# Seven block products for eight in twelve pairs of column groups of a float32 decoder layer

## The chip, the core and the metric

The kernel runs on one core of one Trainium2 chip, in one launch. The metric is the device time of that launch in microseconds (us). TensorE (PE in the profile; PEld is its weight load) multiplies, VectorE (DVE), ScalarE (ACT) and GpSimd (POOL) do the rest, and SyncE (SP) issues nearly all DMAs. Each engine takes its instructions in the order in which they were written; engines wait for each other through semaphores.

## The reference, cut to what matters

One decoder layer for 256 tokens of width 2048, in float32. All large products have the 256 tokens on one side and a weight matrix on the other; the change touches the products for the three gates (3 x 2048 of the columns of `w_in`) and for the SwiGLU input (`w_ffn_in`, 2 x 5632 columns).

```python
h = rms_norm(x, g_pre_mix)
proj = h @ w_in                                  # q, k, v, indexer, ..., gate_logits
o_a = dsa_attention(...); o_b = retention(...); o_c = memory_attention(...)
gates = sigmoid(gate_logits).reshape(B, S, 3, D)
mixed = gates[..0] * (o_a @ w_branch_a) + gates[..1] * (o_b @ w_branch_b) + gates[..2] * (o_c @ w_branch_c)
x = x + rms_norm(mixed @ w_out, g_post_mix)
h2 = rms_norm(x, g_pre_ffn)
f_gate, f_up = split(h2 @ w_ffn_in)
x = x + rms_norm((silu(f_gate) * f_up) @ w_ffn_out, g_post_ffn)
```

## The kernel before

**The split.** A float32 product is made of three products of a shorter type (fp32r): each operand is cut into a high part and a low part (the rest), and x.w = xh.wh + xh.wl + xl.wh. The activations are cut once (`Operand.hi`, `Operand.lo`, transposed, k in the partitions); the weights are cut as they stream past.

**Jobs, chunks, units.** `jobs` is one list of column groups, mostly 512 columns wide, in the order of the program. A job (`Job`, L71) takes `kt` blocks of 128 in k: 16 for a projection of width 2048, 8 for the branches a and c, 44 for the last product. A chunk is four of these blocks, 1 MB of weights, loaded by one DMA into a `raw` tile (three buffers, L127). A unit is half a chunk: ScalarE casts 128x1024 weights to `whi` (L140), VectorE subtracts to get `wlo` (L146), and TensorE does twelve matmuls of 512 columns: two k blocks times two halves of the tokens times three products (L204 to L206), into the job's two accumulators of a PSUM bank each.

**Order.** The instruction order is written out by hand by `Stream.run` (L150): ahead of unit s it writes the casts up to unit s+3 and the subtractions up to unit s+2 (`for kind, ahead in ((his, 3), (los, 2))`, L178), casts first. `whi` and `wlo` have four buffers each, so a cast for unit s+3 writes over what unit s-1 has read. After each unit, `tick` (L112) takes one step of each of two queues of side work: `fast`, the evacuations of the jobs' accumulators, and `slow`, everything else (attention, retention, residual). `until` (L118) takes as many steps as are needed where a unit needs something that has not been written yet. `turned` (L367) transposes an evacuated group through VectorE's 32x32 transposes, eight small DMAs to DRAM and one back, and two more steps some units later; `transpose_split` (L414) does it with TensorE transposes.

**What stands around the change.** Order of the jobs: four of the memory, three of the indexer, two each of aq, ak, av, mq, rq and rk (all with xs, the normalised tokens); then ga 0, branch a 0, ga 1, branch a 1, and so on to 3; the same with gc and branch c; four times rg and rv (retention, each followed by `retain` in the slow queue); gb and branch b; four of `w_out`; then eleven times a gate and an up group of the SwiGLU (`ffn_gate` L1028, `ffn_up` L1039; xop is h2), and four of `w_ffn_out`. The evacuation of a merge (L755) takes two multiplications with a bank and two additions; that of rk (`roped_T`, `rope` L468) four operations per half of the tokens and a `turned`. `make_h2` (L958) makes h2 beside the first SwiGLU job and then puts `residual` (L1002, six steps) into the slow queue. PSUM is two pools of four banks: the jobs' accumulators (`acc`) and all else (`aux`).

```python
for kind, ahead in ((his, 3), (los, 2)):
    h = len(kind)
    if h >= 2 * loaded or h > s + ahead or (kind is los and h >= len(his)):
        continue
    if h > s and h >= 4 and last_use[h - 4] > n - 1:
        continue
```

Of the kernel before, what the change touches and what calls it, by code (L numbers as in the profile page):

```python
# [19 lines left out]
P = 128  # L20
D = 2048
S = 256
# [6 lines left out]
NF = DFF // 512  # L29
TOPK = 64  # L30
# [24 lines left out]
class Operand:  # L55


    def __init__(self):
        self.hi, self.lo, self.ready = [], [], set()
# [29 lines left out]

class Stream:  # L90


    def __init__(self, nc, wr, ws, acc, nm):
        self.nc, self.wr, self.ws, self.acc, self.nm = nc, wr, ws, acc, nm
        self.fast, self.slow = deque(), deque()
        self.now, self.calls = 0, []

# [29 lines left out]
    def load(self, job, c, pieces):  # L127
        raw = self.wr.tile([P, 4, job.nw], F32, tag="raw", name=self.nm("raw"))
        flat = raw.rearrange("p a b -> p (a b)")
        n = 4 * job.nw // pieces  # L130
        for k in range(pieces):
            if 2 * k % pieces == 0:
                job.xop.load(c, 2 * k // pieces)
            self.nc.sync.dma_start(flat[:, k * n:(k + 1) * n], job.w[c][:, k * n:(k + 1) * n])
        return raw

    def high(self, raw, hf, nw, pieces=1):
        hi = self.ws.tile([P, 2, nw], F32R, tag="whi", name=self.nm("whi"))
        for sl in ([slice(0, 2)] if pieces == 1 else [slice(0, 1), slice(1, 2)]):
            self.nc.scalar.copy(hi[:, sl], raw[:, 2 * hf + sl.start:2 * hf + sl.stop])  # L140
        return hi

    def low(self, raw, hf, nw, hi, pieces=1):
        lo = self.ws.tile([P, 2, nw], F32R, tag="wlo", name=self.nm("wlo"))
        for sl in ([slice(0, 2)] if pieces == 1 else [slice(0, 1), slice(1, 2)]):
            self.nc.vector.tensor_sub(lo[:, sl], raw[:, 2 * hf + sl.start:2 * hf + sl.stop],  # L146
                                      hi[:, sl].bitcast(F32))
        return lo

    def run(self, jobs):  # L150
        PE = self.nc.tensor
        chunks = [(j, c) for j in jobs for c in range(j.kt // 4)]
        units = []
        base = 0
        for j in jobs:
            nch = j.kt // 4
            c = 0
            while c < nch:
                both = (j.lead == "first" and c == 0) or (j.lead == "last" and c == nch - 2)
                for group in ([(0,), (1,)] if both else [(0, 1)]):  # L160
                    for cc in range(c, c + 2 if both else c + 1):
                        for hf in range(2):
                            units.append((j, cc, hf, group, 2 * (base + cc) + hf))
                c += 2 if both else 1
            base += nch
        last_use = {u[4]: n for n, u in enumerate(units)}
        raws, his, los, order = {}, {}, {}, []
        loaded = 0
        for n, (j, c, hf, group, s) in enumerate(units):
            while loaded < len(chunks) and loaded <= s // 2 + 3:  # L170
                if loaded >= 3 and 2 * (loaded - 3) + 1 >= len(los):
                    break
                raws[loaded] = self.load(*chunks[loaded], (4, 2, 2, 2)[loaded] if loaded < 4 else 1)
                loaded += 1
            more = True
            while more:
                more = False
                for kind, ahead in ((his, 3), (los, 2)):  # L178
                    h = len(kind)
                    if h >= 2 * loaded or h > s + ahead or (kind is los and h >= len(his)):  # L180
                        continue
                    if h > s and h >= 4 and last_use[h - 4] > n - 1:
                        continue
                    jj, cc = chunks[h // 2]
                    raw = raws[h // 2]
                    if kind is los:
                        los[h] = self.low(raw, h % 2, jj.nw, his[h], 2 if h < 2 else 1)
                    else:
                        jj.xop.ahead(cc, h % 2)
                        his[h] = self.high(raw, h % 2, jj.nw, 2 if h < 2 else 1)  # L190
                    more = True
            if c == 0 and hf == 0 and 0 in group:
                self.until(lambda: len(order) < 2 or order[-2].done)
                order.append(j)
                j.ps = [self.acc.tile([P, j.nw], F32, tag="acc", name=self.nm("acc")) for _ in range(2)]
            self.until(lambda: all((c, m) in j.xop.ready for m in group))
            hi, lo = his[s], los[s]
            for q in range(2):
                k = 4 * c + 2 * hf + q
                first, last = k == 0, k == j.kt - 1  # L200
                for m in group:
                    xh = j.xop.hi[c][:, 2 * hf + q, m * P:(m + 1) * P]
                    xl = j.xop.lo[c][:, 2 * hf + q, m * P:(m + 1) * P]
                    PE.matmul(j.ps[m], xh, hi[:, q], start=first, stop=False)  # L204
                    PE.matmul(j.ps[m], xh, lo[:, q], start=False, stop=False)  # L205
                    PE.matmul(j.ps[m], xl, hi[:, q], start=False, stop=last)  # L206
            if k == j.kt - 1:
                if j.per_m:
                    for m in group:
# [966 lines left out]
```

## Time and profile before

| | us |
|---|---|
| median of 3 runs | 1894.98 (1894.8 to 1895.67) |
| the profiled execution, its own time | 1893.63 |
| its span, from the first to the last instruction | 1891.9 |
| TensorE busy in it | 1879.8 |
| VectorE busy | 1084.8 |
| ScalarE busy | 850.8 |

The profile is one execution, recorded by the hardware. Busy is the time in which an engine had an instruction of its own running; matmuls overlap, so the distance between the starts of two of them, not their duration, is what one costs. Idle time is put down to whatever ended it.

### The profile page before, as it was taken

What the parts mean: (1) busy time and instruction counts of PE and PEld (TensorE: products, weight loads), DVE (VectorE), ACT (ScalarE), POOL (GpSimd) and SP (SyncE); (2) the same over time, 40 slices, a digit from 0 to 9 for tenths busy, and PEclk for the clock granted to TensorE, in tenths of its full rate; (3) what the DMA queues carried; (4) which work ended last, traced back from release to release, by engine and by line L of the source; (5) the groups of instructions that cost most, each with busy time, mean ns of one, the idle gap of its engine ahead of it and who ended that gap; (6) DMA issues with size and microseconds to landing.
All of it is one profiled execution on the core that took longest, in us unless ns stands there. A gap on an engine that the chain in (4) does not pass through costs nothing.

```text
span 1891.9 us, 21493 instructions
## 1 busy us (share of the span) xinstructions
PE 1879.8 (99%) x8436; PEld 1555.0 (82%) x8436; DVE 1084.8 (57%) x1308; ACT 850.8 (45%) x994; POOL 26.9 (1%) x41
## 2 busy tenths in 40 slices
PE   9999999999999999999999999999999999999998
PEld 7888878888888888888888887888888888888886
DVE  5666767765445554555555666655555555544444
ACT  7634444545444444444444444544444444444442
POOL 0000000000000000000100000000000000000000
PEclk9999999999999999999999999999999999999999
DMA  9857656555555556555566664666566666665553
GB/s 345 300 185 253 229 196 219 184 186 199 190 198 192 191 195 223 195 197 199 202 220 233 221 224 157 227 217 222 206 217 223 214 214 230 220 215 197 200 185 127
DMA packets 98134, 399.54 MB, mean 211 GB/s; under 512 B 11104, under 2 KB 43360, under 8 KB 56560
## 3 DMA queue, kind: packets, MB, share of 16 engines
q1 hardware_dynamic: 96864, 394.97, 59.4%
q0 software_dynamic: 1024, 3.18, 0.7%
q8 instruction: 66, 1.08, 0.2%
q14 instruction: 36, 0.29, 0.0%
q10 hardware_dynamic: 144, 0.01, 0.0%
HBM read 379.77 MB, written 18.35 MB: 210 GB/s over the span
## 4 chain that ended last, share of the span: by engine, by line
PE 97%; DVE 1%; DMA 1%; issue 0%; ACT 0%; POOL 0%; POOLq 0%; DVEq 0%; SPq 0%; ACTq 0%
PE acc L204 31%; PE acc L205 31%; PE acc L206 31%; DMA raw<-in_w_iq 1%; DVE wlo L146 0%; PE bk L697 0%; PE bk L715 0%; PE bk L589 0%; PE bk L662 0%; DMA raw<-in_w_mem_kv 0%; PE bk L682 0%; PE bk L816 0%; PE bk L815 0%; PE bk L814 0%; PE bk L802 0%
## 5 line engine op out<-in xcount | busy, mean ns | idle before, releaser
L146 DVE TENSOR_TENSOR wlo<-raw,whi 128x1024 fp32r<-128x1024 f32 (+2 forms) x674 | 810.5, 1208 | 557.4 <-ACT whi L140 555.7
L140 ACT CAST whi<-raw 128x1024 fp32r<-128x1024 f32 (+2 forms) x674 | 701.9, 1042 | 887.2 <-PE acc L206 822.1
L204 PE MATMUL acc<-whi,hi 128*128 128x512 f32 (+2 forms) x2688 | 1049.0, 390 | 0.4 <-ACT whi L140 0.4
L205 PE MATMUL acc<-wlo,hi 128*128 128x512 f32 (+2 forms) x2688 | 1041.6, 388 | 0.7 <-DVE wlo L146 0.6
L206 PE MATMUL acc<-whi,lo 128*128 128x512 f32 (+2 forms) x2688 | 1041.4, 387 | 0.0
L204 PEld LDWEIGHTS acc<-whi,hi 128*128 128x128 f32 x2688 | 505.5, 188 | 104.1 <-ACT whi L140 1.3
L205 PEld LDWEIGHTS acc<-wlo,hi 128*128 128x128 f32 x2688 | 505.4, 188 | 103.5 <-DVE wlo L146 2.6
L206 PEld LDWEIGHTS acc<-whi,lo 128*128 128x128 f32 x2688 | 505.1, 188 | 103.0
L412 DVE TENSOR_TENSOR lo<-turned,hi 128x1024 fp32r<-128x1024 f32 x17 | 20.8, 1226 | 42.0 <-ACT hi L411 39.0
L759 DVE TENSOR_TENSOR gate<-gate,acc 128x512 f32<-128x512 f32 x24 | 16.4, 684 | 29.3 <-PE acc L206 29.3
L1043 DVE SCALAR_TENSOR_TENSOR fg<-acc,rstd,fg 128x512 f32<-128x512 f32 x22 | 16.5, 748 | 26.8 <-PE acc L206 26.8
L477 DVE TENSOR_TENSOR rp<-acc,cos 128x512 f32<-128x512 f32 (+2 forms) x24 | 14.5, 604 | 21.8 <-PE acc L206 21.8
L825 POOL TENSOR_TENSOR rs<-ve,mhalf 128x2 f32<-128x2 f32 x8 | 12.5, 1557 | 814.0 <-DVE ve L823 814.0
L750 ACT ACTIVATE gate<-acc,rstd 128x512 f32<-128x512 f32 x24 | 16.5, 686 | 9.9 <-PE acc L206 9.9
L363 ACT CAST hi<-bk 128x512 fp32r<-128x512 f32 x12 | 7.1, 588 | 29.3 <-PE bk L715 11.6
L1034 ACT ACTIVATE fg<-acc,rstd 128x512 f32<-128x512 f32 x22 | 15.1, 686 | 9.9 <-PE acc L206 9.9
L411 ACT CAST hi<-turned 128x1024 fp32r<-128x1024 f32 x17 | 17.8, 1046 | 0.0
L365 DVE TENSOR_TENSOR lo<-bk,hi 128x512 fp32r<-128x512 f32 x12 | 8.3, 688 | 15.5 <-ACT hi L363 15.5
L594 ACT ACTIVATE rel<-bk 128x256 f32<-128x256 f32 (+1 forms) x16 | 7.9, 494 | 18.2 <-PE bk L589 18.2
L806 DVE TENSOR_TENSOR sT<-bk,dec 128x256 f32<-128x256 f32 x8 | 3.4, 424 | 21.8 <-PE bk L803 21.8
L820 DVE BATCH_NORM_STATS2 bst<-bk 128x6 f32<-128x256 f32 x16 | 6.7, 416 | 15.3 <-PE bk L816 15.3
L478 DVE TENSOR_TENSOR rp<-acc,sin 128x512 f32<-128x512 f32 (+2 forms) x24 | 14.4, 598 | 0.0
(156 smaller groups left out, 468.4 us busy)
## 6 DMA issues: line engine op xcount, KB each, us to landing
raw<-in_w_in SPq DMA_DIRECT2D x132, 1024.0 KB, 4.8
raw<-in_w_ffn_in SPq DMA_DIRECT2D x88, 1024.0 KB, 4.8
raw<-in_w_ffn_out SPq DMA_DIRECT2D x44, 1024.0 KB, 4.8
raw<-in_w_branch_b SPq DMA_DIRECT2D x16, 1024.0 KB, 5.3
raw<-in_w_out SPq DMA_DIRECT2D x16, 1024.0 KB, 4.8
d<-y SPq DMA_DIRECT2D x248, 64.0 KB, 3.1
turned<-d SPq DMA_DIRECT2D x31, 512.0 KB, 5.5
raw<-in_w_mem_kv SPq DMA_DIRECT2D x12, 1024.0 KB, 7.2
```

What stands on the lines that cost most here:

```text
L140: self.nc.scalar.copy(hi[:, sl], raw[:, 2 * hf + sl.start:2 * hf + sl.stop])
L146: self.nc.vector.tensor_sub(lo[:, sl], raw[:, 2 * hf + sl.start:2 * hf + sl.stop], hi[:, sl].bitcast(F32))
L204: PE.matmul(j.ps[m], xh, hi[:, q], start=first, stop=False)
L205: PE.matmul(j.ps[m], xh, lo[:, q], start=False, stop=False)
L206: PE.matmul(j.ps[m], xl, hi[:, q], start=False, stop=last)
L411: A.copy(h4, v)
L412: V.tensor_sub(l4, v, h4.bitcast(F32))
L477: V.tensor_tensor(t1, s4, cos, op=ALU.mult)
L750: A.activation(t[:, m], ps[m], AF.Sigmoid, scale=rms["x"][:, m:m + 1])
L759: V.tensor_tensor(g[:, m], g[:, m], ps[m], op=ALU.mult)
L1034: A.activation(t[m], ps[m], AF.Silu, scale=rmt["ffn", m])
L1043: V.scalar_tensor_tensor(t[m], ps[m], rmt["ffn", m], t[m], op0=ALU.mult, op1=ALU.mult)
```

## The change

Two neighbouring column groups are made one `Pair`. In one of its four chunks (the first, `cs` = 0), the product is seen as 2 x 2 blocks: two halves of the tokens by two halves of the chunk's k, times two halves of k by the two column groups. Eight block products of six matmuls become seven, by Strassen's scheme in Winograd's form; the other three chunks go as before. `make_forms` makes the four sums of the activations' blocks and cuts them into high and low parts, once for xs and once for h2. The sums of the weights (`t2`, `t3`, `t4`) are made by VectorE in the raw tiles when their high part is cut, and each product is one block of six matmuls into one of four accumulators W, Z, Y, X. Products that belong to two results are shared by copying an accumulator to SBUF while it goes on growing (`snapshot`, ScalarE); `finish` adds the copy to the accumulator (VectorE) and hands the sum to the old evacuation.

Pairs are ga 0 and 1, ga 2 and 3, the same of gc and gb, and gate and up group of SwiGLU 1 to 6. The merges of two groups now follow the pair. A block counts half a unit for the side queues. Raw buffers go from three to five, the pool of working tiles from 32 to 31, the two PSUM pools become one of eight, the third group merged with branch b is transposed by TensorE, and the DMA scratch is set to 4096.

```diff
+BLOCKS = range(1, 7)
...
+    def plan_pair(self, pr):
+        (j1, j2), xop, cs = pr.jobs, pr.xop, pr.cs
+        nch = j1.kt // 4
+        nc, V, A = self.nc, self.nc.vector, self.nc.scalar
+        loads = {(g, c): Load(j.w[c], 512) for g, j in enumerate(pr.jobs) for c in range(nch)}
+        r1, r2 = loads[0, cs], loads[1, cs]
+        rest = [(c, hf) for c in range(nch) if c != cs for hf in range(2)]
+        n = 6 * len(rest)
+        acc = {"W": Acc(j1, 6 + n), "Z": Acc(j1, 6 + n), "Y": Acc(j2, 12 + n), "X": Acc(j2, 18 + n)}
+        used, keep = {}, {}
+        def t2():
+            V.tensor_sub(r1.half(0), r2.half(0), r1.half(0))
+            keep["u"] = self.T([P, 2, 512], n="sum")
+            V.tensor_sub(keep["u"], r2.half(1), r1.half(0))
+            return keep["u"]
+        def t3():
+            V.tensor_sub(r2.half(0), r2.half(1), r2.half(0))
+            return r2.half(0)
+        def t4():
+            V.tensor_sub(r1.half(1), r1.half(1), keep["u"])
+            return r1.half(1)
+        cuts = {1: ([r1], lambda: r1.half(0)), 2: ([r1], lambda: r1.half(1)), 3: ([r2], lambda: r2.half(1)),
+                4: ([r1], t4), 5: ([r1], lambda: r1.half(0)), 6: ([r1, r2], t2), 7: ([r2], t3)}
+        side = {1: ("A", 0, 0), 2: ("A", 1, 0), 3: ("S", 3), 4: ("A", 1, 1), 5: ("S", 0), 6: ("S", 1), 7: ("S", 2)}
+        bank = {1: "X", 2: "W", 3: "Y", 4: "Z", 5: "Y", 6: "X", 7: "X"}
+        def snapshot(a, g, m):
+            def take():
+                if g not in pr.snap:
+                    pr.snap[g] = self.T([P, 2, 512], n="snap")
+                A.copy(pr.snap[g][:, m], acc[a].tile)
+                acc[a].read = True
+            return take
+        taken = {1: snapshot("X", 0, 0), 6: snapshot("X", 1, 0), 7: snapshot("X", 0, 1), 5: snapshot("Y", 1, 1)}
+        def parts(i):
+            if side[i][0] == "A":
+                _, hf, m = side[i]
+                return lambda q: [t[cs][:, 2 * hf + q, m * P:(m + 1) * P] for t in (xop.hi, xop.lo)]
+            return lambda q: [t[:, side[i][1], q] for t in xop.forms[cs]]
+        def block(i):
+            ls, cut = cuts[i]
+            s = self.add_item(ls, 512, cut, used[{6: 1, 4: 2}[i]] if i in (4, 6) else -1)
+            used[i] = s
+            a = acc[bank[i]]
+            self.add_unit(Unit(s, [(a, parts(i))], lambda: cs in xop.forms, 0.5,
+                               begin=lambda: self.begin(a), end=taken.get(i)))
+        def plain(g, c, hf, end=None):
+            l = loads[g, c]
+            s = self.add_item([l], 512, lambda: l.half(hf))
+            two = [acc[a] for a in ("WZ", "YX")[g]]
+            def stat(m):
+                return lambda q: [t[c][:, 2 * hf + q, m * P:(m + 1) * P] for t in (xop.hi, xop.lo)]
+            def begin():
+                for a in two:
+                    self.begin(a)
+            self.add_unit(Unit(s, [(two[m], stat(m)) for m in range(2)],
+                               lambda: all((c, m) in xop.ready for m in range(2)), begin=begin, end=end))
+        def finish(g):
+            def evac():
+                j, t = pr.jobs[g], pr.snap[g]
+                for m, a in enumerate(("WZ", "YX")[g]):
+                    V.tensor_add(t[:, m], acc[a].tile, t[:, m])
+                    if m == 0:
+                        yield
+                j.done = True
+                yield "free"
+                yield from j.evac([t[:, m] for m in range(2)])
+            return lambda: self.fast.append(evac())
+        gap = max(1, (len(rest) - 2) // 4)
+        first, second = list(rest), list(rest)
+        def some(g, left, k):
+            for _ in range(k):
+                c, hf = left.pop(0)
+                plain(g, c, hf, None if left else finish(g))
+        block(1)
+        for i in (2, 6, 7, 4):
+            block(i)
+            some(0, first, gap)
+        block(5)
+        some(0, first, len(first))
+        some(1, second, 1)
+        block(3)
+        some(1, second, len(second))
+        self.add_loads(loads.values())
...
+    def begin(self, a):
+        if a.tile is None:
+            self.until(lambda: sum(b.live for b in self.accs) <= 4)
+            self.open([a], 512)
...
+        for n, unit in enumerate(self.units):
+            s = unit.s
             more = True
             while more:
                 more = False
+                while loaded < len(loads) and loads[loaded].first <= s + 6:
+                    if sum(l.last >= len(los) for l in loads[:loaded]) >= (3 if loaded < 8 else self.RAWS):
+                        break
+                    self.load(loads[loaded], (4, 2, 2, 2)[loaded] if loaded < 4 else 1)
+                    loaded += 1
                 for kind, ahead in ((his, 3), (los, 2)):
                     h = len(kind)
+                    if h >= len(items) or h > s + ahead or (kind is los and h >= len(his)):
                         continue
+                    if h > s and h >= 4 and items[h - 4].last_use > n - 1:
                         continue
+                    it = items[h]
                     if kind is los:
+                        los.append(self.low(srcs[h], it.nw, his[h], 2 if h < 2 else 1))
+                    elif it.after >= len(los) or any(where[id(l)] >= loaded for l in it.loads):
+                        continue
                     else:
+                        srcs.append(it.cut())
+                        his.append(self.high(srcs[h], it.nw, 2 if h < 2 else 1))
                     more = True
+            if unit.begin:
+                unit.begin()
+            self.until(unit.ready)
             hi, lo = his[s], los[s]
             for q in range(2):
+                for a, parts in unit.muls:
+                    xh, xl = parts(q)
+                    for x, w in ((xh, hi), (xh, lo), (xl, hi)):
+                        held = unit.end is not None and q == 1 and w is hi and x is xl
+                        a.n += 1
+                        PE.matmul(a.tile, x, w[:, q], start=a.n == 1,
+                                  stop=a.n == a.total or held, skip_group_check=a.read)
+            if unit.end:
+                unit.end()
+            passed += unit.weight
+            while passed >= 1:
+                passed -= 1
+                self.tick()
         while self.fast or self.slow or self.calls:
             self.tick()
...
-    tp = ctx.enter_context(tc.tile_pool(name="tp", bufs=32))
+    tp = ctx.enter_context(tc.tile_pool(name="tp", bufs=31))
     hp = ctx.enter_context(tc.tile_pool(name="hp", bufs=8))
-    wr = ctx.enter_context(tc.tile_pool(name="wr", bufs=3))
+    wr = ctx.enter_context(tc.tile_pool(name="wr", bufs=Stream.RAWS))
     ws = ctx.enter_context(tc.tile_pool(name="ws", bufs=4))
     sm = ctx.enter_context(tc.tile_pool(name="sm", bufs=4))
-    acc = ctx.enter_context(tc.tile_pool(name="acc", bufs=4, space=bass.MemoryType.PSUM))
-    aux = ctx.enter_context(tc.tile_pool(name="aux", bufs=4, space=bass.MemoryType.PSUM))
+    ps = ctx.enter_context(tc.tile_pool(name="ps", bufs=8, space=bass.MemoryType.PSUM))
...
+    def make_forms(op, c):
+        while not {(c, 0), (c, 1)} <= op.ready:
+            yield "wait"
+        f, g = T([P, 4, S], n="whole"), T([P, 4, 2, P], n="forms")
+        V.tensor_add(f, op.hi[c].bitcast(F32), op.lo[c].bitcast(F32))
+        yield
+        a11, a12, a21, a22 = (f[:, 2 * k:2 * k + 2, m * P:(m + 1) * P] for m in range(2) for k in range(2))
+        V.tensor_add(g[:, 0], a21, a22)
+        V.tensor_sub(g[:, 1], g[:, 0], a11)
+        yield
+        V.tensor_sub(g[:, 2], a11, a21)
+        V.tensor_sub(g[:, 3], a12, g[:, 1])
+        yield
+        hi, lo = T([P, 4, 2, P], F32R, "fhi"), T([P, 4, 2, P], F32R, "flo")
+        A.copy(hi, g)
+        yield
+        V.tensor_sub(lo, g, hi.bitcast(F32))
+        op.forms[c] = hi, lo
...
+    def pair():
+        two = jobs.pop()
+        jobs.append(Pair(jobs.pop(), two))
...
+    def then_forms(evac):
+        def both(ps):
+            yield from evac(ps)
+            yield from make_forms(xs, 0)
+        return both
     for i in range(2):
-        proj("rk", i, roped_T(straight(rkT)))
+        e = roped_T(straight(rkT))
+        proj("rk", i, then_forms(e) if i else e)
...
+    def gates_of(name, xop, w, kt, then=None):
+        for i in (0, 2):
+            gate(name, i)
+            gate(name, i + 1)
+            pair()
+            merge(name, i, xop, w[i], kt, then)
+            merge(name, i + 1, xop, w[i + 1], kt, then)
+    gates_of("ga", oa, io["w_branch_a"], 8)
+    gates_of("gc", oc, io["w_branch_c"], 8)
...
-        if i < 3:
+        if i < 2:
...
+    gates_of("gb", ob, io["w_branch_b"], KD, after_merge)
...
-        st.slow.append(residual())
+        st.slow += [residual(), make_forms(h2, 0)]
...
         jobs.append(Job(h2, io["w_ffn_in"][2 * j + 1], KD, 512, ffn_up(j)))
+        if j in BLOCKS:
+            pair()
...
-    nc = bacc.Bacc("TRN2", target_bir_lowering=False, num_devices=1)
+    nc = bacc.Bacc("TRN2", target_bir_lowering=False, num_devices=1, dynamic_dma_scratch_size=4096)
```

## Rows read from the trace of the kernel before

**Rows 1.** Page, part 1: engine, busy us, share of the span, instructions.
```profile
PE 1879.8 (99%) x8436; PEld 1555.0 (82%) x8436; DVE 1084.8 (57%) x1308; ACT 850.8 (45%) x994; POOL 26.9 (1%) x41
```
**Rows 2.** Page, part 4: the chain of work that ended last, by engine.
```profile
PE 97%; DVE 1%; DMA 1%; issue 0%; ACT 0%; POOL 0%; POOLq 0%; DVEq 0%; SPq 0%; ACTq 0%
```
**Rows 3.** Waits of TensorE, one of six: waited for, us in total, times, longest.
```profile
PE acc L205 <- DVE wlo L146: 0.6, 3, 0.3
```
**Rows 4.** Timeline in the SwiGLU: start us, us, engine, instruction, [idle before, releaser].
```profile
1302.48 0.39 PE L204 MATMUL acc<-whi,hi 128*128 128x512 f32 x1
...
1303.84 0.39 PE L204 MATMUL acc<-whi,hi 128*128 128x512 f32 x1
...
1304.04 1.05 ACT L140 CAST whi<-raw 128x1024 fp32r<-128x1024 f32 x1 [1.67 <-PE acc L206]
...
1305.13 1.23 DVE L146 TENSOR_TENSOR wlo<-raw,whi 128x1024 fp32r<-128x1024 f32 x1 [1.49 <-ACT whi L140]
...
1305.20 0.39 PE L204 MATMUL acc<-whi,hi 128*128 128x512 f32 x1
```
**Rows 5.** Groups by line and shape: count, busy us, mean ns, idle before, releaser.
```profile
L146 DVE TENSOR_TENSOR wlo<-raw,whi 128x1024 fp32r<-128x1024 f32 x654 | 796.0, 1222 | 549.2 <-ACT whi L140 547.4 <-DMA d<-y 1.5
L140 ACT CAST whi<-raw 128x1024 fp32r<-128x1024 f32 x654 | 688.9, 1054 | 868.7 <-PE acc L206 811.2 <-DVE gate L759 16.6 <-DMA raw<-in_w_mem_kv 13.1
...
L412 DVE TENSOR_TENSOR lo<-turned,hi 128x1024 fp32r<-128x1024 f32 x17 | 20.8, 1226 | 42.0 <-ACT hi L411 39.0 <-PE acc L205 3.0
...
L1043 DVE SCALAR_TENSOR_TENSOR fg<-acc,rstd,fg 128x512 f32<-128x512 f32 x22 | 16.5, 748 | 26.8 <-PE acc L206 26.8
L759 DVE TENSOR_TENSOR gate<-gate,acc 128x512 f32<-128x512 f32 x24 | 16.4, 684 | 29.3 <-PE acc L206 29.3
...
L373 DVE STREAM_TRANSPOSE y<-fg 128x512 f32<-128x512 f32 x22 | 14.3, 687 | 0.0
...
L477 DVE TENSOR_TENSOR rp<-acc,cos 128x512 f32<-128x512 f32 x18 | 12.4, 688 | 21.4 <-PE acc L206 21.3
...
L479 DVE TENSOR_TENSOR rot<-rp,rp 128x256 f32<-128x256 f32 x18 | 7.7, 425 | 0.6
...
L363 ACT CAST hi<-bk 128x512 fp32r<-128x512 f32 x12 | 7.1, 588 | 29.3 <-PE bk L715 11.6 <-PE bk L684 10.2 <-PE bk L358 7.5
```
**Rows 6.** Timeline beside the making of h2, columns as in group 4.
```profile
1164.92 1.22 DVE L146 TENSOR_TENSOR wlo<-raw,whi 128x1024 fp32r<-128x1024 f32 x1
...
1166.19 0.50 PE L205 MATMUL acc<-wlo,hi 128*128 128x512 f32 x1 [0.18 <-DVE wlo L146]
```
**Rows 7.** Single lines: durations in ns, first and last start in us.
```profile
L715 PE MATMUL bk<-pTm,mv x32: 377/379/379, 420.4 to 461.5; 128*128 128x256 f32 x32
...
L750 ACT ACTIVATE gate<-acc,rstd x24: 682/687/690, 467.0 to 1051.2; 128x512 f32<-128x512 f32 x24
...
L1006 DVE SCALAR_TENSOR_TENSOR xr<-yg,rstd,xr x6: 744/744/747, 1184.7 to 1190.3; 128x512 f32<-128x512 f32 x6
```
**Rows 8.** Timeline around four transposes by TensorE, columns as in group 4.
```profile
1167.45 0.60 PE L941 MATMUL bk<-ident,ygg 128*128 128x128 f32 x4
...
1167.81 0.48 PE L204 MATMUL acc<-whi,hi 128*128 128x512 f32 x1
```
**Rows 9.** Timeline of the first matmuls of the span, columns as in group 4.
```profile
1.19 4.45 PE L263 MATMUL bk<-zero 128*128 128x512 bf16 x10 [1.19 <-DVE zero L258]
...
9.95 0.63 PE L206 MATMUL acc<-whi,lo 128*128 128x512 f32 x1
...
10.37 0.46 PE L204 MATMUL acc<-whi,hi 128*128 128x512 f32 x1
...
10.67 0.40 PE L205 MATMUL acc<-wlo,hi 128*128 128x512 f32 x1
...
10.91 0.39 PE L206 MATMUL acc<-whi,lo 128*128 128x512 f32 x1
```
**Rows 10.** Busy time by stretch: us, then PE, PEld, DVE, ACT, POOL (count), PEclk, DMA share, GB/s.
```profile
8.00:10.00 2.00, 2.00 (x7) 1.52 (x6) 1.78 (x4) 1.49 (x4) 0.00 (x0) 1.00 0.99 327
```

More of the change, by code (lines that the diff above doesn't have):

```diff
@@ L87, in evacuate, with __init__, live, half @@
         self.done = True
+class Pair:
+    def __init__(self, one, two, cs=0):
+        self.jobs, self.xop, self.cs, self.snap = (one, two), one.xop, cs, {}
+class Acc:
+    def __init__(self, job, total):
+        self.job, self.total, self.n, self.tile, self.read = job, total, 0, None, False
+    @property
+    def live(self):
+        return self.tile is not None and not self.job.done
+class Load:
+    def __init__(self, w, nw, before=None):
+        self.w, self.nw, self.before = w, nw, before
+        self.first, self.last, self.raw = None, None, None
+    def half(self, hf):
+        return self.raw[:, 2 * hf:2 * hf + 2]
+class Item:
+    def __init__(self, loads, nw, cut, after=-1):
+        self.loads, self.nw, self.cut, self.after, self.last_use = loads, nw, cut, after, None
+class Unit:
+    def __init__(self, s, muls, ready, weight=1.0, begin=None, end=None):
+        self.s, self.muls, self.ready, self.weight = s, muls, ready, weight
+        self.begin, self.end = begin, end
 class Stream:
-    def __init__(self, nc, wr, ws, acc, nm):
-        self.nc, self.wr, self.ws, self.acc, self.nm = nc, wr, ws, acc, nm
+    RAWS = 5
+    def __init__(self, nc, wr, ws, acc, nm, T):
+        self.nc, self.wr, self.ws, self.acc, self.nm, self.T = nc, wr, ws, acc, nm, T
         self.fast, self.slow = deque(), deque()
         self.now, self.calls = 0, []
+        self.loads, self.items, self.units, self.accs = [], [], [], []
     def call(self, units, fn):
@@ L137, in high, with add_item, add_loads, add_unit @@
-    def high(self, raw, hf, nw, pieces=1):
+    def add_item(self, loads, nw, cut, after=-1):
+        s = len(self.items)
+        self.items.append(Item(loads, nw, cut, after))
+        for l in loads:
+            l.first = s if l.first is None else l.first
+            l.last = s
+        return s
+    def add_loads(self, loads):
+        self.loads += sorted(loads, key=lambda l: l.first)
+    def add_unit(self, unit):
+        self.items[unit.s].last_use = len(self.units)
+        self.units.append(unit)
@@ new lines, in open, with load @@
+    def open(self, accs, nw):
+        for a in accs:
+            a.tile = self.acc.tile([P, nw], F32, tag="bank", name=self.nm("acc"))
+            self.accs.append(a)
+        self.accs = [a for a in self.accs if a.live or a in accs]
+    def begin(self, a):
+        if a.tile is None:
+            self.until(lambda: sum(b.live for b in self.accs) <= 4)
+            self.open([a], 512)
+    def load(self, l, pieces):
+        l.raw = self.wr.tile([P, 4, l.nw], F32, tag="raw", name=self.nm("raw"))
+        flat = l.raw.rearrange("p a b -> p (a b)")
+        n = 4 * l.nw // pieces
+        for k in range(pieces):
+            if l.before and 2 * k % pieces == 0:
+                l.before(2 * k // pieces)
+            self.nc.sync.dma_start(flat[:, k * n:(k + 1) * n], l.w[:, k * n:(k + 1) * n])
@@ L153, in run @@
[L153 to L174, printed above, removed]
+        loads, items = self.loads, self.items
@@ L175, in run @@
+        where = {id(l): i for i, l in enumerate(loads)}
+        srcs, his, los = [], [], []
+        loaded, passed = 0, 0.0
+        for n, unit in enumerate(self.units):
+            s = unit.s
             more = True
@@ L191, in run @@
                     more = True
[L192 to L196, printed above, removed]
+            if unit.begin:
+                unit.begin()
+            self.until(unit.ready)
             hi, lo = his[s], los[s]
             for q in range(2):
[L199 to L206, printed above, removed]
@@ L248, in bank @@
     def bank(shape):
-        return aux.tile(shape, F32, tag="aux", name=nm("bk"))
+        return ps.tile(shape, F32, tag="bank", name=nm("bk"))
     def small(shape, n="s", bufs=3):
         return sm.tile(shape, F32, tag=f"{n}{math.prod(shape[1:])}", name=nm(n), bufs=bufs)
-    st = Stream(nc, wr, ws, acc, nm)
+    st = Stream(nc, wr, ws, ps, nm, T)
     zero = T([P, 512], mybir.dt.bfloat16, n="zero")
```

81 lines of the change are left out of this document (44 added, 37 removed).

## The prediction, before the change was run

> **What bounds the kernel now.** Read the busy table first: TensorE is busy 1879.8 us of a span of 1891.9, VectorE 1084.8 [rows 1]. A pipelined matmul can look busy while it waits, so the chain of work that ended last comes next: 97% of it is TensorE [rows 2]. The waits of TensorE alone come third: all its waits on VectorE's low halves add up to 0.6 us in the whole span [rows 3]. So matmuls run back to back, and the time is their number times their spacing. The timeline gives it: twelve matmuls (one half chunk, called a unit below) take 1305.20 - 1302.48 = 2.72 us, 0.2267 us each [rows 4]. The other reading that matters is how far ahead the helpers may run. There are four whi and four wlo buffers, so ScalarE's cast for unit s+3 starts only when unit s-1 has ended (its idle is ended by TensorE, 0.2 us after the slot of the last matmul, 1303.84 to 1304.04), and VectorE's subtraction follows it at once [rows 4]. VectorE idles over half the time in such a stretch and still can't get further ahead; and each engine takes its instructions in the order in which they were written.
>
> **What the change removes.** A pair replaces eight block products of one chunk by seven, each six matmuls of 512 columns, the shape that is there now: 6 x 0.2267 = 1.36 us a pair, for twelve pairs **-16.3 us**, all on the bounding engine. That is the most it can give.
>
> **What it adds, by engine.** Per pair VectorE gets three more low halves and four more subtractions of the same shape (T2 takes two, T3 and T4 one each), 7 x 1.222 us, and four additions of a snapshot to a bank (0.684 each, the row of the gate times acc product) [rows 5]: 11.3 us. A pair of SwiGLU groups now costs VectorE 16 x 1.222 + 2 x 0.748 + 2 x 0.687 + 1.226 = 23.6 us in 43.5 us of matmuls [rows 5]; it will cost 35 in 42.2. On average that fits. ScalarE gets 3 x 1.054 and four snapshots at 0.588 [rows 5], 5.5 us, on 16 x 1.054 and a turned chunk before, 25 in 42 us with the rest: it fits too and I cost it at nothing (its cover is its own idle time; were that gone, its part of the bunch would cost as much as VectorE's).
>
> **Where the addition lies.** It is bunched: five of seven blocks stand in the first 17.7 us of a pair, each lasts TensorE only 1.36 us but costs VectorE a full 1.222, with T2 to T4 on top and the previous job's evacuation in the same queue. Count from T0, the end of the last unit ahead of the pair; VectorE cannot start the evacuation before T0 + 0.2. Units follow as b1 b2 p1 b6 p2 b7 p3 b4 p4 b5 (b a block, p a half of another chunk). In the order written, with TensorE wanting each low half at the unit's second matmul:
> - first evacuation step 0.69, T2 2.44, low of p1 1.22: done at 4.55. TensorE wants it at 2.72 + 0.23 = 2.95: 1.6 late. T2 is written ahead of it because high halves are cut three items ahead and low halves two.
> - low of b6 1.22, second step 0.69, T3 1.22, low of p2 1.22: 8.9, wanted 7.03, 1.9 late.
> - third step 0.75, low of b7, T4, low of p3: 13.3, wanted 11.1, 2.2 late.
> - fourth step 0.75, lows of b4 and p4: 16.5, wanted 15.2; from here VectorE catches up.
> What has been waited for once isn't waited for again, so the pair's stall is the largest of these, **2.2 us**. A block counts half a step for the side queues, so seven leave half a step over, and in every other pair the fourth step comes ahead of p3's low half: 2.95. Mean 2.6, against 1.36 saved. That TensorE does stop in such a place, and goes on 0.05 us after the subtraction ends, is seen once: low half 1164.92 + 1.22, matmul at 1166.19 [rows 6]. Merge evacuations (four steps of 0.685) give the same within 0.3.
>
> **Ten ordinary pairs: +26.** Lower bound 16 (only the first lag counts, the rest is caught up), upper 38 (one more 1.226 us subtraction of a turned chunk or of the last retention heads falls into the bunch; the second gb pair has this).
>
> **First gates pair: +12.5.** make_forms is appended to the evacuation of the job right ahead of it, and b1 may not be written before the forms are. So rope's four steps for m=0 (2 x 0.69 + 2 x 0.425 = 2.2), T2, low of p1 end at 6.1 (wanted 2.95: 3.1 late); then rope for m=1 2.2, two transposes 1.37, the whole 1.22, four 256-wide forms 1.7, ScalarE's cast 1.05, the forms' low 1.22 and only then b6's low 1.22: 16.1 [rows 5]. TensorE, having waited 3.1, has been done with p1 since 8.6: 7.3 more. T3 and p2's low put 1.1 on top, and cross-attention steps, which run until 461 us while the gates begin near 445 (first evacuation at 467 less one job of 21.8), about 1 [rows 7]. Bounds 7 (the forms' second half hidden by b2 and p1) and 17.
>
> **First SwiGLU pair: +4.7.** Its forms come behind residual (six steps) in the slow queue, and residual starts at 1184.7 [rows 7], one unit ahead of the up job; four of the five forms steps are out when the pair begins, the last (1.22) with the rest of the up evacuation (0.75, 1.37) and b6's low are forced ahead of b6: 9.2 after T0, where TensorE is ready at 7.4. 1.75 + 1.8 + 1.1 for the same bunch behind it. Bounds 3 and 8.
>
> **Smaller terms.** One more merged group is turned by TensorE (two groups of four transposes, each pushing the next matmul from 1167.45 to 1167.81 [rows 8]): +0.7, for nine small DMAs on SyncE, which nobody waits for. The 7 us idle spell may cost clock: at the start of the span, after idle, matmuls begin 0.42 us apart from 1.19 to 10.37 us (512 columns at the 1.2 GHz level) and 0.24 apart from 10.67 (2.4), while the granted clock column reads 1.00 for that stretch too [rows 9, 10]. A second such spell, 9 us at half rate, would cost 4.5; I take +1.5, for the one idle spell of that length. Five raw buffers instead of three, and eight shared banks instead of four and four: 0, since loads are hidden and TensorE's waits name none of them; at most -0.6 on the one side [rows 3] and, on the other, rival 3.
>
> **Sum:** -16.3 + 26 + 12.5 + 4.7 + 0.7 + 1.5 = +29.1. The profiled execution took 1893.6 (span 1891.9), so 1922.7; the median of the runs lies 1.35 above it: **1924 us**. With all lower bounds (16, 7, 3, 0.7, 0) it is +10.4, 1905; with all upper ones (38, 17, 8, 0.7, 4.5) +52, 1947.
>
> **Rivals.**
> 1. VectorE's extra work is covered, and the change is faster: if p1's low half and not T2 comes first in VectorE's queue, or two units of lead (5.4 us) are really there at T0, the bunch of 21 us of VectorE work in 18 us of matmuls is nearly absorbed, and 16.3 less some 5 for the forms gives 1879 to 1884. For it: VectorE is 57% busy now [rows 1]. Against: the order written, and buffers that hold it back [rows 4]. It decides from a stall of 1.36 us a pair. Chance 0.08, 0.01 of it within 0.2% of before.
> 2. Only the first lag of each pair counts, and the forms are mostly hidden: 12 x 1.6 + 8 - 16.3, near +11 to +13, 1906. Against: T3 and T4 stand right behind. Chance 0.14, of which 0.04 within 0.2% of before, should the forms be hidden as well (12 x 1.6 - 16.3 = +3).
> 3. A new wait for storage: accumulators and helper tiles rotate over the same eight banks, and the working tiles are one fewer with up to five more alive; an instruction that takes a tile just freed by a late VectorE step holds its engine. One wait of 1.2 us (a subtraction) a pair gives +14 more: 1938. Against: TensorE has no such wait now [rows 3]. Chance 0.12.
> 4. The clock falls at every pair: twelve spells of 2 to 3 us idle, each followed by matmuls 0.43 apart instead of 0.23. At a fifth of the start's cold time, 2 us, that is 12 x 1 = +12; at all of it +55: 1936 to 1979. Against: rows of the 2.4 level go on after the one stop at 1166 us, but that was under half a us [rows 6, 8]. Chance 0.07. The Trainium skill, "TensorE: Matmul & The Clock Gate", Part 1, says that an idle TensorE falls to 1.2 GHz by default and that only sustained activity brings 2.4 back; by that rule the spell of 7 us does cost, at most the 4.5 of the upper bound, and the sum would be 1927; no run here shows an idle spell of that kind in mid-kernel.
> 5. The change doesn't save the 72 matmuls' time, because six matmuls in a row into one bank go slower than two times three: three in a row already go at 0.2267 [rows 4]. Chance 0.01.
>
> **Chances.** The forecast 0.58 (1912 to 1934), rivals as given. Measurements of this kernel tell 0.2%, 3.8 us, from no change: faster 0.07, same 0.05, slower 0.88. The range that leaves out rival 1, the lower end of rival 2 and the upper end of rival 4 is 1905 to 1945.
>
> **What would show it.** In the profile after: 72 fewer matmuls (8 more transposes); TensorE's waits with the low-half line on top, near 45 us, in places about 5 and 11 us behind the start of each pair; one wait of 7 us near 450 us at b6; VectorE near 1228 us busy (1084.8 + 12 x 11.3 + 8 for the forms); spacing of 0.2267 inside units. Wrong if TensorE's waits stay under 16 us, if they name ScalarE or storage, or if matmuls stand 0.43 apart behind them.

## The result

| | before | after |
|---|---|---|
| median of the runs, us | 1895.33 (4 runs) | 1909.17 (4 runs, 1907.33 to 1909.69) |
| ratio, with its 95% interval | | 1.007 (1.0053 to 1.0088) |
| span of the profiled execution, us | 1891.9 | 1907.9 |

The change makes the kernel slower by 13.8 us, where 29 were forecast. The sign, the place and the engine were right; the size was twice too large.

The page after, part 1 (engine, busy us, share of the span, instructions) and part 4 (the chain by engine):

```profile
PE 1874.0 (98%) x8372; PEld 1541.1 (81%) x8372; DVE 1212.6 (64%) x1451; ACT 908.8 (48%) x1081; POOL 27.5 (1%) x41
...
PE 90%; DVE 6%; issue 2%; DMA 1%; ACT 1%; SPq 0%; POOL 0%; POOLq 0%; DVEq 0%; ACTq 0%
```

Against [rows 1, 2]: 64 matmuls fewer (72 less, 8 transposes more), VectorE 128 us busier, and VectorE has gone from 1% to 6% of the chain that sets the end. The two largest waits of TensorE (waited for, us in total, times, longest), where [rows 3] had 0.6:

```profile
PE acc L417 <- DVE wlo L371: 16.0, 24, 2.1
PE acc L417 <- ACT snap L276: 4.7, 1, 4.7
```

This view counts from the end of the last matmul's modelled duration. What a stop costs is the distance between the starts of two matmuls less 0.2267. Taken so over the whole trace, the span's +16.0 us divides as follows:

| term | forecast | trace after |
|---|---|---|
| 72 matmuls less | -16.3 | -16.3 |
| ten ordinary pairs | +26 | +12.8 |
| first gates pair, half clock in it | +12.5 + 1.5 | +8.8 |
| first SwiGLU pair | +4.7 | +3.0 |
| half clock in the second gb pair | 0 | +1.4 |
| transposes by TensorE | +0.7 | +1.0 |
| the rest: delays under 0.12 us each, waits at the start and in the indexer's jobs | 0 | +5.3 |

Of the last row 2.4 stand right behind 22 of the stops, where the next distance is 0.34 instead of 0.2267; 1.3 lie in the indexer's jobs, 0.8 at the start.

The 12.8 are nine stops of 0.85 and one of 1.38 at p1, and second stops of 0.29, 0.42, 0.41, 0.40 and (second gb pair) 2.29. The timeline at the head of SwiGLU pair 3 (start us, us, engine, instruction, [idle before, releaser]), VectorE first, then TensorE:

```profile
1311.37 0.69 DVE L314 TENSOR_TENSOR snap<-acc,snap 128x512 f32<-128x512 f32 x1 [2.45 <-PE acc L417]
1311.97 1.22 DVE L254 TENSOR_TENSOR raw<-raw,raw 128x1024 f32<-128x1024 f32 x1
1313.22 1.23 DVE L256 TENSOR_TENSOR sum<-raw,raw 128x1024 f32<-128x1024 f32 x1
1314.37 1.22 DVE L371 TENSOR_TENSOR wlo<-raw,whi 128x1024 fp32r<-128x1024 f32 x1
...
1317.38 1.22 DVE L260 TENSOR_TENSOR raw<-raw 128x1024 f32<-128x1024 f32 x1
1318.52 1.22 DVE L371 TENSOR_TENSOR wlo<-raw,whi 128x1024 fp32r<-128x1024 f32 x1
1319.65 0.75 DVE L1288 SCALAR_TENSOR_TENSOR fg<-snap,rstd,fg 128x512 f32<-128x512 f32 x1
1320.32 1.22 DVE L371 TENSOR_TENSOR wlo<-raw,whi 128x1024 fp32r<-128x1024 f32 x1
...
1322.59 1.22 DVE L371 TENSOR_TENSOR wlo<-raw,whi 128x1024 fp32r<-128x1024 f32 x1
...
1314.57 0.39 PE L417 MATMUL acc<-whi,hi 128*128 128x512 f32 x1
1315.64 0.50 PE L417 MATMUL acc<-wlo,hi 128*128 128x512 f32 x1 [0.69 <-DVE wlo L371]
```

The reader sees the forecast's queue, instruction for instruction: first evacuation step, T2's two, p1's low half, and TensorE's second matmul of p1 starting 0.05 us after it. p1's first matmul stands two blocks (2.72) behind T0, so T0 is 1311.85. Two things are not as forecast. The evacuation step starts 0.48 us **ahead** of T0. And the instructions are closer than they are long: from 1317.38 to 1318.52 are 1.14 us for one of 1.22, from 1319.65 to 1320.32 0.67 for one of 0.75 (not from 1311.97 to 1313.22, where the second needs the first's result: 1.25).

### The profile page after: what moved, and what is told of

It is laid out like the page before. It is cut to its first block, busy times and chain, and to the rows that moved or that the text cites. A ratio compares the mean times of both kernels' runs of the same rounds, so it can differ in the third digit from the quotient of the medians.

```text
span 1907.9 us, 21599 instructions
## 1 busy us (share of the span) xinstructions
PE 1874.0 (98%) x8372; PEld 1541.1 (81%) x8372; DVE 1212.6 (64%) x1451; ACT 908.8 (48%) x1081; POOL 27.5 (1%) x41
## 4 chain that ended last, share of the span: by engine, by line
PE 90%; DVE 6%; issue 2%; DMA 1%; ACT 1%; SPq 0%; POOL 0%; POOLq 0%; DVEq 0%; ACTq 0%
PE acc L417 87%; DVE wlo L371 2%; DVE raw L254 1%; DMA raw<-in_w_mem_kv 1%; ACT whi L365 0%; DMA raw<-in_w_iq 0%; PE bk L951 0%; PE bk L825 0%; DVE raw L260 0%; DVE sum L256 0%; PE bk L933 0%; DVE raw L264 0%; DVE y L583 0%; PE bk L898 0%; DVE rp L708 0%
## 5 line engine op out<-in xcount | busy, mean ns | idle before, releaser
L371 DVE TENSOR_TENSOR wlo<-raw,whi 128x1024 fp32r<-128x1024 f32 (+2 forms) x698 | 837.9, 1208 | 424.1 <-ACT whi L365 420.1
L365 ACT CAST whi<-raw 128x1024 fp32r<-128x1024 f32 (+2 forms) x698 | 724.7, 1042 | 801.1 <-PE acc L417 715.8
L417 PE MATMUL acc<-wlo,hi 128*128 128x512 f32 (+2 forms) x2568 | 997.7, 389 | 14.2 <-DVE wlo L371 13.8
L417 PE MATMUL acc<-whi,hi 128*128 128x512 f32 (+2 forms) x2568 | 1002.5, 390 | 1.9 <-ACT whi L365 1.9
L417 PE MATMUL acc<-whi,lo 128*128 128x512 f32 (+2 forms) x2568 | 995.1, 388 | 0.0
L314 DVE TENSOR_TENSOR snap<-acc,snap 128x512 f32<-128x512 f32 x48 | 33.0, 688 | 48.0 <-PE acc L417 48.0
L417 PE MATMUL acc<-whi,fhi 128*128 128x512 f32 x96 | 38.6, 402 | 4.7 <-ACT snap L276 4.7
L417 PE MATMUL acc<-wlo,fhi 128*128 128x512 f32 x96 | 38.1, 397 | 2.2 <-DVE wlo L371 2.2
L417 PE MATMUL acc<-whi,flo 128*128 128x512 f32 x96 | 37.9, 395 | 0.0
L276 ACT COPY snap<-acc 128x512 f32<-128x512 f32 x48 | 27.9, 582 | 5.8 <-PE acc L417 5.8
L1072 POOL TENSOR_TENSOR rs<-ve,mhalf 128x2 f32<-128x2 f32 x8 | 12.5, 1558 | 826.7 <-DVE ve L1070 826.7
```

Source lines behind the costliest of these rows:

```text
L276: A.copy(pr.snap[g][:, m], acc[a].tile)
L314: V.tensor_add(t[:, m], acc[a].tile, t[:, m])
L365: self.nc.scalar.copy(hi[:, sl], src[:, sl])
L371: self.nc.vector.tensor_sub(lo[:, sl], src[:, sl], hi[:, sl].bitcast(F32))
L417: PE.matmul(a.tile, x, w[:, q], start=a.n == 1, stop=a.n == a.total or held, skip_group_check=a.read)
L1072: G.tensor_tensor(rs, ve, mhalf[:, :2], op=ALU.pow)
```

## The experiments

Each kernel is the changed one with the edit shown. Ratios are to the kernel before, run beside it.

**1. Is it the pairs at all?** Three kernels: no pairs, only the gates', only the SwiGLU's.

```diff
-BLOCKS = range(1, 7)
+BLOCKS = ()                                   # no pairs; only the gates' pairs
-            pair()                             # gates_of: no pairs; only the SwiGLU's pairs
```
The forms that no pair uses are left out too.

> No pair and no forms; the rest of the change stays (five raw buffers, one pool of eight banks, gates two by two, one group more turned by TensorE). Theory (the loss comes from VectorE's bunched work in the pairs): near the kernel before, 1895.3 + 0.7 for the transposes + up to 3 of small waits at the start that the trace after shows, 1896 to 1899, and TensorE's waits for low halves under 3 us. Rival (the rearrangement itself costs the time): 1903 or more.

Measured: 1895.87 us, ratio 1.0006 (0.9997 to 1.0016), waits for low halves 1.0 us. The buffers, the shared banks and the new order of the jobs cost nothing that can be measured. The forecast's rival 3 (storage) falls for these; the tiles that only a pair uses are left to experiment 2.

> Pairs in the gates only (six). Theory: their stops in the trace after add up to 8.8 (first pair) + 8.8 + 1.4 of half clock = 19, less 8.2 saved: the time of the kernel without pairs + 10 to 11, about 1907. Rival (all pairs cost alike): half of what separates no pairs from twelve, + 6.

Measured: 1905.72, 1.0057 (1.0041 to 1.0074): +9.9.

> Pairs in the SwiGLU only (six). Theory: stops of 3.0 (first pair) + 5.5 (five others), less 8.2 saved: even, the time of the kernel without pairs within 1 us, about 1898. Rival (all pairs cost alike): + 6.

Measured: 1897.71, 1.0015 (1.0006 to 1.0025): +1.8, a little more than even. Most of the loss lies in the gates: 9.9 of the 13.3 us between no pairs and all (the SwiGLU alone 1.8, the rest only together). So pairs do not cost alike, and the loss is not in the seven products themselves, which are the same in both.

**2. VectorE's sums taken away.**

```diff
-            V.tensor_sub(r1.half(0), r2.half(0), r1.half(0))     # t2, and so for t3 and t4
-            keep["u"] = ...; V.tensor_sub(keep["u"], r2.half(1), r1.half(0))
-            return keep["u"]
+            return r2.half(1)
```

> All pairs, but the four sums of weights per pair (T2, T3, T4) are left out and the blocks take unsummed halves, so this is the time without 48 VectorE subtractions. Theory (VectorE's queue at the head of a pair): the stops of 0.85 to 2.3 us in the eleven later pairs go, 12.8 + 1.4 + some 2 of the first SwiGLU pair, while the 7 us at b6 in the first gates pair shrink by about 2.4 at most: 1893 to 1897. Rival (snapshots, banks or ScalarE hold TensorE): within 4 us of 1909.

Measured: 1886.11, 0.9955 (0.994 to 0.9969). Without the sums the kernel computes another product, so only its time counts. It is 7 us better than the expectation, which had subtracted from 1909 the stops it named. In the trace the first gates pair also loses 3.1 of its 8.8, the first SwiGLU pair all of its 3.0, and the delays under 0.12 us are 3.0 less, 2.0 of it directly behind stops. Left are 4.3 us at b6 in the first gates pair with 1.4 of half clock behind them, and 0.5 in the second gb pair. Snapshots, banks and ScalarE, which this kernel still has, hold TensorE in no other pair.

**3. Does VectorE really start ahead of T0?** A unit takes its matmuls as first half of the tokens, second half, first, second, three each. The first accumulator is therefore complete 3 x 0.2267 = 0.68 us ahead of the unit's end. Adding the second one first should take that lead away.

```diff
-                for m, a in enumerate(("WZ", "YX")[g]):
+                for m, a in ((1, "ZX"[g]), (0, "WY"[g])):
```

> finish adds the second accumulator (second half of the tokens) first. In a unit the first accumulator's last matmul lies three matmuls, 0.68 us, ahead of the second's, so VectorE's queue would begin that much later behind each pair. Theory (the prediction's first lag was too long because VectorE starts 0.68 us earlier than T0 + 0.2): the wait at p1 of SwiGLU pairs 2 to 6 grows from 0.85 to 1.5, 5 x 0.68 = +3.4 in all, about 1912.5. Rival (0.85 comes from shorter subtractions alone): 0.85 as before, 1909.

Measured: 1911.33, 1.0085 (1.0072 to 1.0099). The time itself moved by 2.2, where 3.4 was expected and runs of one kernel differ by about 2; the trace settles it. TensorE at p1 of SwiGLU pair 3, columns as above:

```profile
1314.06 0.39 PE L417 MATMUL acc<-whi,hi 128*128 128x512 f32 x1
1315.81 0.50 PE L417 MATMUL acc<-wlo,hi 128*128 128x512 f32 x1 [1.36 <-DVE wlo L371]
```

1.75 between the two starts where it was 1.07: +0.68, in each of the five pairs.

**4. What does one VectorE instruction cost in a full queue?** One more subtraction of the same shape ahead of T2.

```diff
+            V.tensor_sub(keep["u"], r2.half(1), r2.half(0))
             V.tensor_sub(r1.half(0), r2.half(0), r1.half(0))
```

> One more subtraction of 128x1024 ahead of T2 in each pair (its result is overwritten by T2). Theory (the wait at p1 is VectorE's queue, and one instruction of such a queue costs its distance to the next, 1.14 us, not its 1.222): the wait at p1 of SwiGLU pairs 2 to 6 grows from 0.85 to 1.99; some 1.14 x 11 or a little less (where a later lag had been larger) in all, 1919 to 1922. Rival (1.222 counts): 2.07 there. Rival (VectorE has slack at p1): 0.85 there and 1909.

Measured: 1925.15, 1.016 (1.0145 to 1.0175). The same place:

```profile
1324.48 0.39 PE L418 MATMUL acc<-whi,hi 128*128 128x512 f32 x1
1326.69 0.50 PE L418 MATMUL acc<-wlo,hi 128*128 128x512 f32 x1 [1.82 <-DVE wlo L372]
```

2.21 against 1.07: +1.14, in nine of the ordinary pairs, and +1.13 in the tenth. Its distance to the next instruction counts, not its duration. The total rose by 16, not by 10 to 13 as expected; the profiled execution was 14.4 longer than that of the change. The two first pairs wait 1.1 more each as well, and the clock fell behind two of the longer stops, near 660 and 1281 us, where in the change it fell once.

**5. p1's low half ahead of T2.**

```diff
-                for kind, ahead in ((his, 3), (los, 2)):
+                for kind, ahead in ((los, 2), (his, 3)):
```

> Low halves are written ahead of the next high half, so p1's low half comes before T2 on VectorE. One theory (only T2 ahead of p1's low half matters): the waits at p1 go, 11 x 0.85 saved, 1899 or less. Other theory (VectorE's whole chain counts: T2 now ends later, then ScalarE's cast of 1.05, then b6's low half, one behind the other with VectorE idle between): p1 doesn't wait, but b6 and b7 do, by 0.5 and 1.2 us in each pair and more in the first ones, so it is slower, 1915 to 1922.

Measured: 1923.05, 1.0148 (1.0134 to 1.0162), so the forecast's rival 1 in this form falls. p1 doesn't stop any more; b6 and b7 do, by 0.55 and 1.15 in the regular pairs. (b7's first matmul waits for the snapshot of b6's accumulator, which stands in ScalarE's queue behind the cast of T3.) VectorE, ScalarE and TensorE around b6 of one:

```profile
1321.84 1.23 DVE L256 TENSOR_TENSOR sum<-raw,raw 128x1024 f32<-128x1024 f32 x1
...
1323.18 1.05 ACT L365 CAST whi<-sum 128x1024 fp32r<-128x1024 f32 x1 [5.28 <-DVE sum L256]
...
1324.27 1.23 DVE L371 TENSOR_TENSOR wlo<-sum,whi 128x1024 fp32r<-128x1024 f32 x1 [1.20 <-ACT whi L365]
...
1324.77 0.50 PE L417 MATMUL acc<-whi,fhi 128*128 128x512 f32 x1
1325.55 0.50 PE L417 MATMUL acc<-wlo,fhi 128*128 128x512 f32 x1 [0.27 <-DVE wlo L371]
```

VectorE now idles 1.20 us behind T2 until ScalarE has cut the sum: in the order of the change p1's low half fills just this hole.

**6. The forms made early.**

```diff
-        proj("rk", i, then_forms(e) if i else e)
+        proj("rk", i, e if i else then_forms(e))
...
         h2_turn(3, 1)
+        st.slow.append(make_forms(h2, 0))
         yield
...
-        st.slow += [residual(), make_forms(h2, 0)]
+        st.slow += [residual()]
```

> The forms of xs are made one job earlier (behind rk 0), those of h2 ahead of residual. Theory (the forms on the way to the first block cost 8.8 us in the gates and about 2 in the SwiGLU, half clock behind the first spell included): 1909 - 8 to 10, about 1900; no wait of over 2 us at b6 and no half clock near 455 us. Rival (the first pair's wait comes from cross-attention, which shares VectorE there): not over 3 us better.

Measured: 1898.79, 1.0023 (1.0014 to 1.0033): 10.4 better than the change. In the first gates pair 2.1 us are left at p2's low half and 1.0 ahead of a step of the cross-attention, and there is no half clock; the first SwiGLU pair doesn't stop. In the profiled execution, which took 1897.3, the half clock in the second gb pair is missing too, 1.4 us that are not the forms'.

**7. The blocks spread out,** with a plain unit behind each of six, alone and with the early forms.

```diff
-        block(1)
-        for i in (2, 6, 7, 4):
+        for i in (1, 2, 6, 7, 4, 5):
             block(i)
             some(0, first, gap)
-        block(5)
-        some(0, first, len(first))
```

> The spread order of the blocks alone; the forms stay where the change has them. Theory (density and forms are two separate losses): the ordinary pairs' 12.8 + 1.4 us go but for about 3 in the second gb pair, the first pairs keep most of their 8.8 + 3: 1909 - 10 to 13, 1896 to 1899. Rival (with plain units between, b6 and the forms meet later and that is what helped in the run with both): 1886 to 1889.

Measured: 1895.74, 1.0004 (0.9994 to 1.0014): no ordinary pair stops but the second gb pair (1.07 and 1.97). The two first pairs stop for 6.7 and 2.4, each with half clock behind it. The expectation's two losses are separate: the spread order alone gains 13.4 on the change, the early forms alone 10.4, and both together, next, 24.0.

> Forms early as in the run before, and a plain unit behind each of six blocks (b1 p b2 p b6 p b7 p b4 p b5 p q b3 q...) instead of two blocks in a row at the head. Theory (the loss is VectorE's density at the head of the pair, not its total): the order gives VectorE 4.08 us for each block with its sums and a plain unit, so ordinary pairs don't wait at all: 1895.9 (no pairs) - 16.3 + at most 3 for single places (retention and turned chunks in gb, the first pairs) = 1880 to 1884, faster than both. Rival (VectorE's total work, 84% of a pair, or ScalarE, is what holds it): the waits move to other units and 1895 or more remains.

Measured: 1885.14, 0.9949 (0.9937 to 0.9961): 9.6 us faster than before and 24 faster than the change, one above the range expected. VectorE does the same work as in the change. Page, part 1, of this kernel:

```profile
PE 1867.2 (99%) x8372; PEld 1543.2 (82%) x8372; DVE 1210.4 (64%) x1451; ACT 910.6 (48%) x1081; POOL 26.8 (1%) x41
```

and TensorE's waits for low halves:

```profile
PE acc L414 <- DVE wlo L368: 5.5, 7, 1.8
```

VectorE is as busy as after the change (1210 against 1213), and TensorE waits 5.5 instead of 16.0 for it. So not VectorE's total but its density behind T0, and the forms, are what the change lost. The rest against 1895.9 - 16.3 is three stops (1.7, 1.1, 2.0) and, in the profiled execution, 1.4 us by half clock.

## Why the prediction was right in sign and twice too large

**What bounds, what is removed.** Right: 8372 matmuls, and experiment 7 gets 10.7 of the 16.3 us back against the kernel without pairs.

**The queue behind T0: right in order, wrong in two sizes.** "VectorE cannot start the evacuation before T0 + 0.2" is the step that failed first. It took the end of a unit for the end of its first accumulator, 0.68 us too late (experiment 3). The second is that every VectorE instruction was charged its duration. In a full queue a subtraction costs 1.14 instead of 1.222 (experiment 4), an evacuation step 0.6 to 0.67 instead of 0.69 to 0.75 (timeline above). p1's low half ended at T0 + 3.74 instead of 4.55, that of p2 (1318.52 + 1.22) at 7.9 instead of 8.9, that of p3 (1322.59 + 1.22) at 12.0 instead of 13.3: 0.68 of each is the start, the rest the spacing. With 0.85 waited at p1 TensorE wants the last two at 7.9 and 12.0: they arrive just in time, so that the second and third lags, which made 1.6 into 2.2 to 2.95, vanish but for 0.3 to 0.4 in four of the ten pairs (every other one in the SwiGLU, as the half step said) and the 2.29 of the second gb pair, which the forecast had named for its upper bound. The mean is 1.28 a pair, not 2.6, and the term is 12.8, not 26; it lies below the lower bound that was given for it (16), because both bounds used the same start and the same durations. The number was in the trace of before, had two starts been subtracted instead of two durations added:

```profile
1208.90 1.22 DVE L146 TENSOR_TENSOR wlo<-raw,whi 128x1024 fp32r<-128x1024 f32 x1
1210.03 0.74 DVE L1043 SCALAR_TENSOR_TENSOR fg<-acc,rstd,fg 128x512 f32<-128x512 f32 x1
1210.69 1.22 DVE L146 TENSOR_TENSOR wlo<-raw,whi 128x1024 fp32r<-128x1024 f32 x1
```

The prediction subtracted starts for TensorE, and not for VectorE.

**The first gates pair: the wait at b6 as forecast, that at p1 not.** Timeline of TensorE, ScalarE and VectorE in it:

```profile
441.63 0.48 PE L417 MATMUL acc<-whi,hi 128*128 128x512 f32 x1
...
444.49 1.89 PE L933 MATMUL bk<-turned,qT 128*128 128x256 f32 x8
446.03 0.58 PE L417 MATMUL acc<-whi,hi 128*128 128x512 f32 x1
...
448.88 0.39 PE L417 MATMUL acc<-whi,lo 128*128 128x512 f32 x1
453.93 0.80 PE L417 MATMUL acc<-whi,fhi 128*128 128x512 f32 x1 [4.66 <-ACT snap L276]
455.84 0.79 PE L417 MATMUL acc<-wlo,fhi 128*128 128x512 f32 x1 [1.11 <-DVE wlo L371]
456.43 0.63 PE L417 MATMUL acc<-whi,flo 128*128 128x512 f32 x1
456.86 0.63 PE L417 MATMUL acc<-whi,fhi 128*128 128x512 f32 x1
...
445.19 1.22 DVE L371 TENSOR_TENSOR wlo<-raw,whi 128x1024 fp32r<-128x1024 f32 x1
...
452.35 1.04 ACT L650 CAST fhi<-forms 128x1024 fp32r<-128x1024 f32 x1 [5.94 <-DVE forms L647]
453.30 0.58 ACT L276 COPY snap<-acc 128x512 f32<-128x512 f32 x1
...
453.43 1.23 DVE L652 TENSOR_TENSOR flo<-forms,fhi 128x1024 fp32r<-128x1024 f32 x1 [1.11 <-ACT fhi L650]
454.57 1.22 DVE L371 TENSOR_TENSOR wlo<-sum,whi 128x1024 fp32r<-128x1024 f32 x1
```

At b6 4.83 + 1.68 + 0.37 = 6.9 us are lost (0.2 of it by half clock), 7.3 were forecast, and the chain is the one named: forms, their cast, their low half, b6's low half. The wait carries another name for most of it: the snapshot of b1's accumulator, written behind the forms' cast in ScalarE's queue, is what b6's first matmul waits for. At p1 nothing is lost beyond a handover, where 3.1 was forecast. p1's low half ended 4.78 us behind T0 (441.63) and not 6.1 (its queue began 1.0 sooner than forecast and stood closer by 0.3), and the cross-attention's eight matmuls (444.49 to 446.03, 1.54 us) stand in front of p1 and give VectorE that time. The forecast had booked that attention as one more us of VectorE work and not as work of TensorE that covers. T3 and p2's low half put 0.3 on top, where 1.1 was forecast.

**The first SwiGLU pair:** 0.98 + 1.26 + 0.78 at the three places named, 3.0 for 4.7, which the same two errors of size would do; no run takes it apart.

**The clock.** For the long spell half clock was forecast, and it came. Busy time by stretch (us, PE, PEld, DVE, ACT, POOL, PEclk, DMA share, GB/s):

```profile
453.00:460.00 7.00, 4.81 (x10) 3.00 (x11) 6.43 (x7) 4.89 (x10) 0.00 (x0) 0.52 0.78 251
...
1006.00:1009.50 3.50, 1.37 (x7) 0.90 (x6) 3.50 (x5) 2.18 (x3) 0.00 (x0) 1.00 0.00 0
1009.50:1013.00 3.50, 3.50 (x10) 2.71 (x9) 3.46 (x4) 1.64 (x3) 0.00 (x0) 0.51 0.48 118
```

Between 455.84 and 459.93 the eight distances are 0.43 or more, 0.2 too long each, which costs 1.6; 1.5 was taken. By the Trainium skill, "TensorE: Matmul & The Clock Gate", Part 1, an idle TensorE goes back to 1.2 GHz; the trace agrees, with a granted clock of 0.52 behind this spell. Rival 4 falls as it was put: behind the 0.85 us stops the clock stays at its upper level. But it fell in one place that was not forecast, the second gb pair.

**The rivals.** 1 falls in the form of experiment 5, and is true in the form of experiment 7: VectorE's total can be covered, though not in this order. 2 (only the first lag of each pair counts) was nearest to what happened, at 1906, but by luck: the first lag is half as large, and the forms are not hidden. 3 falls with the kernel without pairs and with the one without sums (experiments 1 and 2). 5 falls: matmuls of a block are 0.2267 apart.

**The signs.** Of those that the forecast gave, the order held: low halves on top, the one long wait near 450 us at b6, 72 matmuls fewer. The sizes did not: 16.0 us of waits for low halves and not 45, VectorE busy 1212.6 and not 1228. And two signs of being wrong showed in part: 4.7 us of wait name ScalarE, and behind two stops matmuls stood 0.43 apart.

## What to carry to other kernels

Charge an instruction of a full queue with the distance between starts, on every engine, and look up in the order of the matmuls when each accumulator is complete: a lag of 1.6 us, worked out from four instructions and a start, was half error. When products are saved at the price of other engines' work, look at the stretch in which that work stands, not at its share of the whole: the same work with a plain unit between the blocks, and with the forms made early, turned a loss of 14 us into a gain of 10. What is needed once (the forms) should not be appended to the last job ahead of its first use.

## What the runs showed of the hardware that was not expected

Two stops of the same length in the same place ended differently. In the changed kernel 2.29 us were lost at 1005.91 in the second gb pair; matmuls started again at 1008.42, 0.23 apart, and only from 1009.77 on were they 0.43 apart, until 1012.75 (granted clock 0.51 in the stretch above). With the early forms 2.26 us were lost in the same pair, and the clock stayed at 1.00:

```profile
998.50:1002.00 3.50, 1.40 (x7) 0.85 (x6) 3.50 (x5) 1.99 (x3) 0.00 (x0) 1.00 0.01 5
1002.00:1006.00 4.00, 4.00 (x19) 3.29 (x18) 4.00 (x5) 3.19 (x5) 0.00 (x0) 1.00 0.48 115
```

With one more sum (experiment 4) nine stops are of the same length, 1.98 us: behind two of them, near 657 and 1279 us, matmuls were 0.43 apart for some 3 us, behind the other seven they were not, nor behind a stop of 2.51 at 910.56. So a stop of about 2 to 2.5 us may or may not cost the clock, its length alone does not decide it, and the half rate begins 0.3 to 1.4 us after TensorE has gone on. It differs between executions of one kernel, too: of the nine of the early forms the three of 1900.8 to 1901.2 us were granted 0.997 of the clock over their span, the two of 1897.3 and 1897.5 us 0.999. Each such spell costs 1.4 us (seven distances, 0.2 each), so differences of that size between two of these kernels may be the clock's alone. What decides it was not tried.
